# Two mixers of a two-layer trunk: subtracts moved from GpSimd to VectorE, queries rotated ahead of their norm, and output projections with two blocks to a bank

## The chip, the cores and the metric

The kernel runs on one core of a Trainium2 chip. A core has five engines, each with its own stream of instructions in a fixed order: TensorE (PE, with its weight load PEld), VectorE (DVE), ScalarE (ACT), GpSimd (POOL) and SyncE (SP, which here issues the DMAs). The metric is the device time of one execution in microseconds (us); lower is better.

## The reference, cut to what matters

A trunk of two layers over 256 tokens of width 1024, all in float32. Layer 0 mixes tokens by differential attention beside stick-breaking attention (one joint input projection, one joint output projection), layer 1 by multi-head latent attention (MLA). Each layer is a half feed-forward, the mixer, cross-attention to a memory of 256 tokens, and another half feed-forward.

```python
for layer in range(DEPTH):                                    # DEPTH = 2
    x = x + 0.5 * swiglu(rms_norm(x, ...), w_gate, w_up, w_down)   # width 2816
    h = rms_norm(x, mix_norm[layer])
    x = x + (diff_stickbreak_mixer(h, ...) if layer % 2 == 0 else mla_mixer(h, ...))
    x = x + memory_cross_attention(rms_norm(x, ...), rms_norm(mem, ...), ...)
    x = x + 0.5 * swiglu(rms_norm(x, ...), ...)
```

In both mixers, the mixed heads are multiplied by an output projection of 1024 x 1024. In MLA a query head is 96 wide; it is normed by its root mean square, and its last 32 values are rotated by their position. A rotation leaves the sum of squares as it is.

## The kernel before, in words

**Three passes.** A float32 product is made from high and low parts: a = hi + lo, and hi·hi + lo·hi + hi·lo is summed in PSUM by three matmuls (`mm3`, lines 285, 286 and 287 of the profile). A weight comes in through an SP DMA into `wr` (two buffers, `RAW`), ACT casts it to `wh` (line 250), and a subtract makes `wl` (line 252). The hi and lo tiles have three buffers (`HL`), so a weight's cast has to wait until PE has read the last of the weight three before it. In the mixers and the cross-attentions a weight of 128 x 2048 is cut into four pieces of 512 columns, p0 to p3, each with its own cast and subtract; DVE makes the subtract of the first three and POOL that of the last (`np_`, 512 columns). In the feed-forwards the pieces have 256 columns and all are DVE's.

**Order.** A planner (`run`) simulates tasks with priorities, tables of estimated durations (`EST_AB`, `EST_MLA`, `EST_X0`, `EST_X1`), times at which weights come and PSUM banks come free, and so fixes PE's order. The other engines' instructions are ordered by the scheduler of the framework; the update of the residual (`finish_dt`: x on DVE at line 511, xh on ACT at 482, xl on DVE at 483) has high priority there. Each engine then goes through its stream in order, and waits where an input or a buffer is not ready.

**Stages.** In us of the span: feed-forward up to 190, mixer of layer 0 ("AB") 190 to 329, its cross-attention to 368, two feed-forwards to 735, MLA 735 to 861, its cross-attention to 900, feed-forward to 1084.

**Output projection.** `out_g` makes eight blocks of 128 output columns out of four chunks of weights, chunk c holding blocks 2c and 2c+1. A block sums over eight rows of 128 (24 matmuls of 256 columns), in groups of two rows as the mixed heads become ready. A first window holds the first three blocks open in three PSUM banks and goes through them group by group, while the rest of the attention is made; then blocks 3 to 7 follow, one after the other. A block that is complete is added to x at once.

**MLA's queries.** `queries` takes each projected group of four heads for 128 tokens (n, t) from PSUM, squares it (ACT), sums the squares (DVE, 1350), adds the epsilon (1351), takes the reciprocal square root on POOL (468, four values a token), and rotates the last 32 values of a head: products with the tables on DVE (1358) and POOL (1360, two instructions), and their sum on DVE (1363). PE then transposes the queries (793), DVE copies them out of PSUM (1435), and the scores follow (1448).

Of the kernel before, what the change touches and what calls it, by code (L numbers as in the profile page):

```python
# [19 lines left out]
P = 128  # L20
S = 256
# [27 lines left out]
POOL_OF = {}  # L49
# [112 lines left out]
def trunk_kernel(ctx, tc, wflat, xT_d, xtok_d, memT_d, memtok_d, gains_d, rows_d, cst_d, out_d):  # L162
# [74 lines left out]
    def issue(i):  # L237
# [4 lines left out]
        np_ = 0 if name in ("gate", "up", "down") else POOL_OF.get(name, 512)  # L242
# [592 lines left out]
    def mem_k(l, c, events):  # L835
# [4 lines left out]
        def norm():  # L840
# [13 lines left out]
            yield dict(t=1, lat=7.0)  # L854
# [371 lines left out]
    def mixer_mla(gc):  # L1226
# [7 lines left out]
        rl, kk, kf, vt, kT, qf, rqs = {}, {}, {}, {}, {}, {}, {}  # L1234
# [103 lines left out]
        def queries(n, t, ps):  # L1338

            yield dict(after=[ev["rcq"]])  # L1340
            if t == 0:
                qf[n], rqs[n] = [], sl()
# [6 lines left out]
            v = sm()[:, 0:4]  # L1349
            V.tensor_reduce(out=v, in_=sq[:, 0:384].rearrange("p (a b) -> p a b", b=96), axis=AX.X, op=ALU.add)  # L1350
# [3 lines left out]
            tmp = al()  # L1354
            m1 = tmp[:, 0:128].rearrange("p (a b) -> p a b", b=32)
# [248 lines left out]
```

## Time and profile before

| | |
|---|---|
| time, median of 3 runs | 1088.73 us (1087.20 to 1089.23) |
| the profiled execution: time, span | 1086.18 us, 1084.5 us |
| busy over the span: PE, DVE, ACT, POOL | 1063.0, 769.4, 655.3, 192.4 us |

The span is what the trace covers; 1.7 us of the profiled execution's time lie around it. Busy time is the union of an engine's instructions, so a PE that is busy is not always at its full pace.

### The profile page before, as it was taken

The page shows a single profiled execution, that of the slowest core. Times are in us where ns is not written, and L with a number is a line of the kernel's source. Part 1 is how long each engine was busy: PE and PEld are TensorE (multiplying, and loading weights), DVE is VectorE, ACT ScalarE, POOL GpSimd, SP SyncE. Part 2 cuts the span into 40 slices and gives each one's busy share as a digit, 9 for nine tenths or more (in the row PEclk, how much of TensorE's full clock was granted, in tenths as well). Part 3 has the DMA queues.
Part 4 walks back from the last instruction along what each step waited for, and adds up shares of the span by engine and source line. Part 5 has one row for each costly group of instructions (what it writes and reads, how often), then busy time and mean ns, then how long its engine had stood idle before and what let it go on. Part 6 is the DMA issues. An engine that isn't in the chain of part 4 may idle for free.

```text
span 1084.5 us, 23380 instructions
## 1 busy us (share of the span) xinstructions
PE 1063.0 (98%) x9034; PEld 1044.5 (96%) x9034; DVE 769.4 (71%) x1866; ACT 655.3 (60%) x1775; POOL 192.4 (18%) x210
## 2 busy tenths in 40 slices
PE   8999999999899999999999999999989999999998
PEld 8999999998799999999999999999878999999998
DVE  5988765567867877776777777664688768777753
ACT  6766565567756665555666655565866567555542
POOL 0200001365434200000100000024861422000000
PEclk9999999999999999999999999999989999999999
DMA  8776556635345355555556565564341444555561
GB/s 285 247 250 218 197 191 206 195 89 184 99 136 195 119 193 196 193 185 199 200 189 220 200 208 184 182 197 158 97 147 49 155 150 164 195 195 195 185 225 58
DMA packets 51232, 193.36 MB, mean 178 GB/s; under 512 B 5808, under 2 KB 8368, under 8 KB 36016
## 3 DMA queue, kind: packets, MB, share of 16 engines
q1 hardware_dynamic: 50976, 191.81, 52.0%
q8 instruction: 71, 1.16, 0.4%
q14 instruction: 41, 0.34, 0.1%
q10 hardware_dynamic: 144, 0.05, 0.0%
HBM read 190.79 MB, written 1.05 MB: 177 GB/s over the span
## 4 chain that ended last, share of the span: by engine, by line
PE 90%; DVE 4%; ACT 2%; POOL 2%; issue 1%; DMA 1%; SPq 0%; DVEq 0%; ACTq 0%; POOLq 0%
PE mm L285 28%; PE mm L286 28%; PE mm L287 28%; DVE wl L252 1%; PE t L793 1%; ACT slotf L780 1%; POOL sm L468 1%; PE s L1448 1%; PE t L476 1%; DMA wr<-wflat 1%; PE s L918 0%; PE o L1481 0%; POOL sl L468 0%; PE s L285 0%; PE o L937 0%
## 5 line engine op out<-in xcount | busy, mean ns | idle before, releaser
L250 ACT CAST wh<-wr 128x256 fp32r<-128x256 f32 (+1 forms) x1216 | 441.0, 434 | 291.6 <-PE mm L286 234.2
L252 DVE TENSOR_TENSOR wl<-wr,wh 128x256 fp32r<-128x256 f32 (+1 forms) x1171 | 479.8, 466 | 125.6 <-ACT wh L250 120.2
L285 PE MATMUL mm<-xh,wh 128*128 128x256 f32 x1552 | 430.5, 277 | 1.9 <-ACT wh L271 1.9
L286 PE MATMUL mm<-xl,wh 128*128 128x256 f32 x1552 | 428.5, 276 | 0.0
L287 PE MATMUL mm<-xh,wl 128*128 128x256 f32 x1552 | 428.2, 276 | 0.0
L285 PEld LDWEIGHTS mm<-xh,wh 128*128 128x128 f32 x1552 | 292.3, 188 | 2.4 <-ACT wh L271 2.1
L286 PEld LDWEIGHTS mm<-xl,wh 128*128 128x128 f32 x1552 | 292.3, 188 | 0.6
L287 PEld LDWEIGHTS mm<-xh,wl 128*128 128x128 f32 x1552 | 292.1, 188 | 0.1
L285 PE MATMUL mm<-slotr,wh 128*128 128x256 f32 x896 | 247.6, 276 | 0.3 <-ACT slotr L482 0.3
L286 PE MATMUL mm<-slotr,wh 128*128 128x256 f32 x896 | 246.7, 275 | 0.4 <-DVE slotr L483 0.4
L287 PE MATMUL mm<-slotr,wl 128*128 128x256 f32 x896 | 246.6, 275 | 0.0
L285 PEld LDWEIGHTS mm<-slotr,wh 128*128 128x128 f32 x896 | 168.2, 188 | 1.0 <-ACT slotr L482 0.6
L286 PEld LDWEIGHTS mm<-slotr,wh 128*128 128x128 f32 x896 | 168.2, 188 | 0.7 <-DVE slotr L483 0.6
L287 PEld LDWEIGHTS mm<-slotr,wl 128*128 128x128 f32 x896 | 168.2, 188 | 0.0
L531 POOL TENSOR_TENSOR acc<-acc,sq 128x256 f32<-128x256 f32 x49 | 38.7, 789 | 452.5 <-ACT sq L523 450.4
L252 POOL TENSOR_TENSOR wl<-wr,wh 128x512 fp32r<-128x512 f32 x45 | 67.3, 1496 | 111.4 <-ACT wh L250 89.2
L739 DVE TENSOR_TENSOR slotf<-mm,rb 128x512 f32<-128x512 f32 x43 | 29.7, 690 | 53.7 <-PE mm L287 53.7
L482 ACT ACTIVATE xh<-x,gains 128x256 fp32r<-128x256 f32 x64 | 32.2, 507 | 27.8 <-DVE x L511 25.8
L780 ACT ACTIVATE slotf<-s,sm,sl 128x256 f32<-128x256 f32 (+1 forms) x64 | 32.7, 521 | 23.1 <-DVE sm L774 17.5
L729 DVE TENSOR_TENSOR slotf<-mm,rb 128x512 f32<-128x512 f32 x43 | 29.6, 689 | 21.0 <-PE mm L287 21.0
L511 DVE SCALAR_TENSOR_TENSOR x<-mm,x 128x256 f32<-128x256 f32 x64 | 26.8, 419 | 23.5 <-PE mm L287 23.5
L483 DVE SCALAR_TENSOR_TENSOR xl<-x,gains,xh 128x256 fp32r<-128x256 f32 x64 | 37.6, 592 | 5.7 <-ACT xh L482 5.5
(204 smaller groups left out, 1196.3 us busy)
## 6 DMA issues: line engine op xcount, KB each, us to landing
wr<-wflat SPq DMA_DIRECT2D x118, 1024.0 KB, 4.9
wr<-wflat SPq DMA_DIRECT2D x179, 256.0 KB, 3.9
wr<-wflat SPq DMA_DIRECT2D x16, 768.0 KB, 4.3
slotf<-memT SPq DMA_DIRECT2D x8, 256.0 KB, 3.4
wr<-wflat SPq DMA_DIRECT2D x2, 512.0 KB, 7.4
slotf<-xtok SPq DMA_DIRECT2D x4, 256.0 KB, 7.1
slotf<-memtok SPq DMA_DIRECT2D x4, 256.0 KB, 4.0
out<-x SPq DMA_DIRECT2D x8, 128.0 KB, 2.0
```

The costliest lines, as they stand in the source:

```text
L250: A.copy(hi[:, a:b], raw[:, a:b])
L252: e.tensor_tensor(out=lo[:, a:b], in0=raw[:, a:b], in1=hi[:, a:b].bitcast(F32), op=ALU.subtract)
L285: PE.matmul(out, a[0], b[0], start=first, stop=False, **kw)
L286: PE.matmul(out, a[0], b[1], start=False, stop=False, **kw)
L287: PE.matmul(out, a[1], b[0], start=False, stop=last, **kw)
L482: return (A.activation(hi, src, AF.Identity, scale=g), V.scalar_tensor_tensor(out=lo, in0=src, scalar=g, in1=hi.bitcast(F32), op0=ALU.mult ...
L483: V.scalar_tensor_tensor(out=lo, in0=src, scalar=g, in1=hi.bitcast(F32), op0=ALU.mult, op1=ALU.subtract))
L511: V.scalar_tensor_tensor(out=xd, in0=ps, scalar=factor, in1=xd, op0=ALU.mult, op1=ALU.add)
L531: G.tensor_tensor(out=st.acc, in0=st.acc, in1=sq, op=ALU.add)
L729: V.tensor_tensor(out=t.rearrange("p (a b) -> p a b", b=S), in0=pg.rearrange("p (a b) -> p a b", b=S), in1=rbb, op=ALU.mult)
L739: V.tensor_tensor(out=u.rearrange("p (a b) -> p a b", b=S), in0=pu.rearrange("p (a b) -> p a b", b=S), in1=rbb, op=ALU.mult)
L780: A.activation(p[:, i * w:(i + 1) * w], sps[:, i * w:(i + 1) * w], AF.Exp, bias=nb[:, i:i + 1], scale=r, accum_out=sums[:, i:i + 1])
```

## The change

Five edits. (1) All four pieces of a mixer's or cross-attention's weight are subtracted by DVE, none by POOL. (2) The first window of `out_g` holds six blocks, two to a bank in three banks; a pair is added to x when both its blocks are complete, and the last two blocks follow one by one (all four output projections of mixers and cross-attentions go through `out_g`). (3) In `queries` the rotation comes ahead of the sum of squares, its two intermediate products lie in unused columns of tiles that are there already, and one reciprocal square root of eight values replaces two of four. (4) Some of the planner's estimates are set anew. (5) In layer 0, the transposes of the memory's keys (`k0`, `k1`), which are made for the cross-attention during the mixer, are planned 9.0 after the projection rather than 7.0.

```diff
-POOL_OF = {}
-EST_X0 = {... 'o': 1.32, 'src': 8.83}
-EST_X1 = {... 'o': 1.18, 'src': 8.83}
-EST_AB = {... 'va': 1.47, ... 'sp': 3.0, ... 'srco': 1.25}
+EST_X0 = {... 'o': 1.6, 'src': 2.0}
+EST_X1 = {... 'o': 1.6, 'src': 2.0}
+EST_AB = {... 'va': 2.8, ... 'sp': 4.4, ... 'srco': 2.2}
...
-        np_ = 0 if name in ("gate", "up", "down") else POOL_OF.get(name, 512)
+        np_ = 0
...
+        nw = 2 * BANKS["mm"]
+        def bank(dt):
+            return dt // 2 * 2 if dt < nw else dt
...
+            b = bank(dt)
+            c0 = (dt - b) * S
             for i, k in enumerate(rows_):
-                mm3(pss[dt][:, 0:S], (w[0][:, k, j * P:(j + 1) * P], w[1][:, k, j * P:(j + 1) * P]),
-                    src[i], g == 0 and i == 0, g == len(groups) - 1 and i == len(rows_) - 1)
+                mm3(pss[b][:, c0:c0 + S], (w[0][:, k, j * P:(j + 1) * P], w[1][:, k, j * P:(j + 1) * P]),
+                    src[i], g == i == 0 and dt == b, g == len(groups) - 1 and i == len(rows_) - 1,
+                    skip_group_check=dt < nw)
...
-                ps = pss.pop(dt)
-                finish_dt(dt, gc, ps[:, 0:S])
-                drop(ps, 0.8)
-        nw = BANKS["mm"]
+                if dt >= nw or dt > b:
+                    for d in range(b, dt + 1):
+                        finish_dt(d, gc, pss[b][:, (d - b) * S:(d - b + 1) * S])
+                    drop(pss[b], 0.8)
...
-            yield dict(t=1, lat=7.0)
+            yield dict(t=1, lat=9.0 if l == 0 else 7.0)
...
-            v = sm()[:, 0:4]
-            V.tensor_reduce(out=v, in_=sq[...], axis=AX.X, op=ALU.add)
-            V.tensor_scalar(out=v, in0=v, scalar1=96 * EPS, scalar2=None, op0=ALU.add)
-            rsqrt(v, 4, rqs[n][:, t * 4:(t + 1) * 4])
...
             V.tensor_tensor(out=qr, in0=m1, in1=m2, op=ALU.add)
-            rel(sq, tmp)
+            V.tensor_reduce(out=qv[n][:, t * 4:(t + 1) * 4], in_=sq[...], axis=AX.X, op=ALU.add)
+            if t:
+                v = qv[n][:, 0:8]
+                V.tensor_scalar(out=v, in0=v, scalar1=96 * EPS, scalar2=None, op0=ALU.add)
+                rsqrt(v, 8, rqs[n])
+            rel(sq)
```

What the change does to the engines' streams shows at three places on DVE. In these rows a name's number is the tile, and the lines of the changed kernel lie 1 lower (up to 650) or 9 to 10 higher than those of the kernel before.

First, DVE in AB around the norm of the memory's first keys, `k0`. Before: lines 1197, 1198 and 1202 norm an attention output (o), 849, 850 and 853 norm `k0`, and POOL's reciprocal square roots stand between 1198 and 1202 and between 850 and 853.

```order
L1197 TENSOR_REDUCE sm_3861<-slotf_2674 128x4
L1164 SCALAR_TENSOR_TENSOR slotf_2658<-slotf_2664,sm_3845 128x256
L1198 TENSOR_SCALAR sm_3861<-sm_3861 128x4
L252 TENSOR_TENSOR wl_3890<-wr_3888,wh_3889 128x512
L1202 TENSOR_TENSOR slotf_2675<-o_3855,sm_3864 128x512
L849 TENSOR_REDUCE sm_3882<-slotf_2673 128x4
L252 TENSOR_TENSOR wl_3890<-wr_3888,wh_3889 128x512
L850 TENSOR_SCALAR sm_3882<-sm_3882 128x4
L252 TENSOR_TENSOR wl_3890<-wr_3888,wh_3889 128x512
L853 TENSOR_TENSOR slotf_2678<-slotf_2678,sm_3885 128x512
```

The changed kernel at the same norm (858, 859 and 862 are its three lines, 1206, 1207 and 1211 those of the attention output):

```order
L251 TENSOR_TENSOR wl_3848<-wr_3846,wh_3847 128x512
L858 TENSOR_REDUCE sm_3840<-slotf_2660 128x4
L251 TENSOR_TENSOR wl_3848<-wr_3846,wh_3847 128x512
L859 TENSOR_SCALAR sm_3840<-sm_3840 128x4
L251 TENSOR_TENSOR wl_3848<-wr_3846,wh_3847 128x512
L862 TENSOR_TENSOR slotf_2658<-slotf_2658,sm_3843 128x512
L251 TENSOR_TENSOR wl_3848<-wr_3846,wh_3847 128x512
L1206 TENSOR_REDUCE sm_3880<-slotf_2664 128x4
L1207 TENSOR_SCALAR sm_3880<-sm_3880 128x4
```

The norm of `k0` now stands ahead of that of the attention output, and four subtracts stand in the place of three.

Second, DVE in MLA from the second group of heads (n=1, both t) to the copies of the first transposed queries. Before:

```order
L1358 TENSOR_TENSOR slotf_9746<-slotf_9733,mqa 128x128
L1350 TENSOR_REDUCE sm_10369<-slotf_9745 128x4
L1363 TENSOR_TENSOR slotf_9733<-slotf_9746 128x4x32
L1351 TENSOR_SCALAR sm_10369<-sm_10369 128x4
L1358 TENSOR_TENSOR slotf_9734<-slotf_9737,mqa 128x128
L252 TENSOR_TENSOR wl_10426<-wr_10424,wh_10425 128x512
L1350 TENSOR_REDUCE sm_10404<-slotf_9742 128x4
L1363 TENSOR_TENSOR slotf_9737<-slotf_9734 128x4x32
L1351 TENSOR_SCALAR sm_10404<-sm_10404 128x4
L252 TENSOR_TENSOR wl_10426<-wr_10424,wh_10425 128x512
L1435 COPY slotf_9743<-t_10461 96x512
```

The changed kernel at the same place (1362, 1367, 1368, 1372 and 1445 are the lines of the product, the rotated sum, the sum of squares, the epsilon and the copy):

```order
L1362 TENSOR_TENSOR slotf_9734<-slotf_9734,mqa 128x128
L1367 TENSOR_TENSOR slotf_9734<-slotf_9734,slotf_9726 128x4x32
L1368 TENSOR_REDUCE sm_10357<-slotf_9726 128x4
L1362 TENSOR_TENSOR slotf_9740<-slotf_9740,mqa 128x128
L251 TENSOR_TENSOR wl_10414<-wr_10412,wh_10413 128x512
L1367 TENSOR_TENSOR slotf_9740<-slotf_9740,slotf_9744 128x4x32
L1368 TENSOR_REDUCE sm_10357<-slotf_9744 128x4
L1372 TENSOR_SCALAR sm_10357<-sm_10357 128x8
L251 TENSOR_TENSOR wl_10414<-wr_10412,wh_10413 128x512 x2
L1445 COPY slotf_9736<-t_10449 96x512
```

The rotation's sum moved ahead of the sum of squares, one epsilon stands for two, and a third subtract has come in ahead of the copy. On POOL, one reciprocal square root of eight values stands where two of four and a subtract stood.

Third, DVE in AB's output projection, from the split of the last mixed heads (483, `slotr`) on. Before, `wl_4098` is the weight of blocks 6 and 7, and `wl_4236` that of the cross-attention's queries:

```order
L483 SCALAR_TENSOR_TENSOR slotr_2682<-t_4143,small,slotr_2682 128x512
L511 SCALAR_TENSOR_TENSOR x<-mm_4082,x 128x256
L511 SCALAR_TENSOR_TENSOR x<-mm_4089,x 128x256
L483 SCALAR_TENSOR_TENSOR xl<-x,gains,xh 128x256
L511 SCALAR_TENSOR_TENSOR x<-mm_4111,x 128x256
L252 TENSOR_TENSOR wl_4098<-wr_4096,wh_4097 128x512
L483 SCALAR_TENSOR_TENSOR xl<-x,gains,xh 128x256 x2
L252 TENSOR_TENSOR wl_4098<-wr_4096,wh_4097 128x512 x2
L511 SCALAR_TENSOR_TENSOR x<-mm_4203,x 128x256
L252 TENSOR_TENSOR wl_4236<-wr_4234,wh_4235 128x512
```

The changed kernel, where `wl_4075` is the weight of blocks 6 and 7, and `mm_4060`, `mm_4088` and `mm_4138` are the banks of blocks 0 and 1, 2 and 3, 4 and 5:

```order
L482 SCALAR_TENSOR_TENSOR slotr_2682<-t_4194,small,slotr_2682 128x512
L510 SCALAR_TENSOR_TENSOR x<-mm_4060,x 128x256 x2
L251 TENSOR_TENSOR wl_4075<-wr_4073,wh_4074 128x512 x2
L510 SCALAR_TENSOR_TENSOR x<-mm_4088,x 128x256 x2
L482 SCALAR_TENSOR_TENSOR xl<-x,gains,xh 128x256
L510 SCALAR_TENSOR_TENSOR x<-mm_4138,x 128x256 x2
L482 SCALAR_TENSOR_TENSOR xl<-x,gains,xh 128x256 x5
L251 TENSOR_TENSOR wl_4075<-wr_4073,wh_4074 128x512 x2
L251 TENSOR_TENSOR wl_4125<-wr_4123,wh_4124 128x512 x4
```

The last two pieces of the last chunk now stand behind six updates of x and six subtracts of xl. In MLA the same stretch reads the same, row for row, with other tile numbers.

## Rows read from the trace of the kernel before

**Rows 1.** The page, parts 1 and 4: busy us (share) xinstructions, and the chain's shares.

```profile
PE 1063.0 (98%) x9034; PEld 1044.5 (96%) x9034; DVE 769.4 (71%) x1866; ACT 655.3 (60%) x1775; POOL 192.4 (18%) x210
...
PE 90%; DVE 4%; ACT 2%; POOL 2%; issue 1%; DMA 1%; SPq 0%; DVEq 0%; ACTq 0%; POOLq 0%
```

**Rows 2.** Windows: stretch, length, busy us (xinstructions) of each engine, PEclk, DMA.

```profile
190.00:320.00 130.00, 123.33 (x1051) 118.44 (x1051) 91.09 (x174) 84.33 (x192) 59.69 (x55) 1.00 0.43 139
...
380.00:735.00 355.00, 355.00 (x3132) 354.95 (x3131) 253.05 (x636) 207.21 (x596) 15.99 (x18) 1.00 0.57 196
735.00:850.00 115.00, 107.80 (x777) 98.24 (x778) 80.39 (x203) 75.91 (x180) 55.65 (x63) 0.97 0.34 111
```

**Rows 3.** Waits of PE, 190 to 320: us in total, times, longest.

```profile
PE t L793 <- DVE slotf L853: 2.3, 1, 2.3
PE s L323 <- ACT slotf L780: 1.9, 2, 1.0
PE o L1105 <- issue: 0.9, 1, 0.9
PE o L1105 <- ACT slotf L1017: 0.9, 1, 0.9
```

**Rows 4.** Waits of PE, whole span.

```profile
PE s L1448 <- DVE slotf L1435: 2.6, 1, 2.6
...
PE o L937 <- DVE slotf L801: 1.1, 2, 0.6
```

**Rows 5.** Timeline 290 to 298, DVE and PE: start, us, what, [idle before <- releaser].

```profile
292.17 0.69 DVE L1202 TENSOR_TENSOR slotf<-o,sm 128x512 f32<-128x512 f32 x1 [0.90 <-POOL sm L468]
292.78 0.68 DVE L849 TENSOR_REDUCE sm<-slotf 128x4 f32<-128x512 f32 x1
...
295.63 1.52 DVE L853 TENSOR_TENSOR slotf<-slotf,sm 128x512 f32<-128x512 f32 x1 [0.90 <-POOL sm L468]
...
297.29 0.63 PE L793 MATMUL t<-cst,slotf 128*128 128x128 f32 x4 [2.27 <-DVE slotf L853]
```

**Rows 6.** Timeline 783 to 792, DVE and PE, at MLA's first queries.

```profile
787.05 0.29 DVE L1363 TENSOR_TENSOR slotf<-slotf 128x128 f32<-128x128 f32 x1 [2.05 <-POOL slotf L1360]
...
789.68 0.29 DVE L1363 TENSOR_TENSOR slotf<-slotf 128x128 f32<-128x128 f32 x1 [1.00 <-POOL slotf L1360]
...
789.96 0.69 DVE L252 TENSOR_TENSOR wl<-wr,wh 128x512 fp32r<-128x512 f32 x1
790.56 1.28 DVE L1435 COPY slotf<-t 96x512 f32<-96x512 f32 x2
...
791.29 1.01 PE L1448 MATMUL s<-slotf,slotf 96*128 96x128 f32 x3 [2.64 <-DVE slotf L1435]
```

**Rows 7.** Windows of 5 us after that wait, columns as in rows 2.

```profile
790.00:795.00 5.00, 3.71 (x13) 3.30 (x14) 3.43 (x6) 2.01 (x4) 4.84 (x4) 0.59 0.39 120
795.00:800.00 5.00, 5.00 (x25) 4.84 (x24) 5.00 (x16) 3.39 (x13) 0.00 (x0) 0.73 0.47 170
```

**Rows 8.** Groups by shape, POOL, whole span: count, busy us, mean ns, idle before.

```profile
L252 POOL TENSOR_TENSOR wl<-wr,wh 128x512 fp32r<-128x512 f32 x45 | 67.3, 1496 | 111.4 <-ACT wh L250 89.2 <-PE mm L286 18.1 <-DMA wr<-wflat 4.1
```

**Rows 9.** Groups by shape, DVE: 190 to 320 (first), 735 to 850 (second).

```profile
L252 DVE TENSOR_TENSOR wl<-wr,wh 128x512 fp32r<-128x512 f32 x52 | 39.6, 793 | 8.3 <-ACT wh L250 8.2
...
L252 DVE TENSOR_TENSOR wl<-wr,wh 128x512 fp32r<-128x512 f32 x35 | 26.8, 784 | 11.9 <-ACT wh L250 11.9
```

**Rows 10.** Timeline 308 to 329, DVE and POOL, in AB's output projection.

```profile
313.46 0.42 DVE L511 SCALAR_TENSOR_TENSOR x<-mm,x 128x256 f32<-128x256 f32 x1 [2.34 <-PE mm L287]
...
315.21 0.68 DVE L252 TENSOR_TENSOR wl<-wr,wh 128x512 fp32r<-128x512 f32 x1
315.81 0.99 DVE L483 SCALAR_TENSOR_TENSOR xl<-x,gains,xh 128x256 fp32r<-128x256 f32 x2
...
321.31 2.98 DVE L252 TENSOR_TENSOR wl<-wr,wh 128x512 fp32r<-128x512 f32 x2 [0.71 <-ACT wh L250]
...
322.40 1.35 POOL L252 TENSOR_TENSOR wl<-wr,wh 128x512 fp32r<-128x512 f32 x1 [0.37 <-ACT wh L250]
```

More of the change, by code (lines that the diff above doesn't have):

```diff
@@ L58 @@
 PREADD = True
-EST_X0 = {'scale': 3.59, 'rq': 1.14, 'psd': 1.46, 'sp': 2.8, 'p1': 4.06, 'p2': 0, 'o': 1.32, 'src': 8.83}
-EST_X1 = {'scale': 2.31, 'rq': 1.14, 'psd': 1.46, 'sp': 2.8, 'p1': 3.39, 'p2': 0.0, 'o': 1.18, 'src': 8.83}
-EST_AB = {'b': 1.33, 'va': 1.47, 'rot': 14.92, 'st1': 6.44, 'st2': 0.14, 'z': 1.55, 'sto': 2.4, 'src': 0.79, 'T': 0.74, 'sp': 3.0, 'pc': 8.7, 'pcT': 1.4, 'po': 4.35, 'oa': 8.7, 'srco': 1.25}
+EST_X0 = {'scale': 3.59, 'rq': 1.14, 'psd': 1.46, 'sp': 2.8, 'p1': 4.06, 'p2': 0, 'o': 1.6, 'src': 2.0}
+EST_X1 = {'scale': 2.31, 'rq': 1.14, 'psd': 1.46, 'sp': 2.8, 'p1': 3.39, 'p2': 0.0, 'o': 1.6, 'src': 2.0}
+EST_AB = {'b': 1.33, 'va': 2.8, 'rot': 14.92, 'st1': 6.44, 'st2': 0.14, 'z': 1.55, 'sto': 2.4, 'src': 0.79, 'T': 0.74, 'sp': 4.4, 'pc': 8.7, 'pcT': 1.4, 'po': 4.35, 'oa': 8.7, 'srco': 2.2}
 PRIO_MLA = [1, 2, 4.2, 3.9, 4.4, 2.3]
@@ L678, in out_g @@
                 for dt in win:
-                    yield dict(after=[ev], w=keyf(dt // per), mm=int(g == 0))
+                    yield dict(after=[ev], w=keyf(dt // per), mm=int(g == 0 and dt == bank(dt)))
                     if dt // per not in ws:
                         ws[dt // per] = weight(keyf(dt // per), per * P)
-                    if g == 0:
+                    if g == 0 and dt == bank(dt):
                         pss[dt] = take("mm")
@@ L1233, in mixer_mla @@
         lat = {"ckv": ([], []), "cq": ([], [])}
-        rl, kk, kf, vt, kT, qf, rqs = {}, {}, {}, {}, {}, {}, {}
+        rl, kk, kf, vt, kT, qf, qv, rqs = {}, {}, {}, {}, {}, {}, {}, {}
         def latent(key, gc0, ps):
@@ L1341, in queries @@
             if t == 0:
-                qf[n], rqs[n] = [], sl()
+                qf[n], qv[n], rqs[n] = [], sm(), sl()
             z = al()
@@ L1348, in queries @@
             A.activation(sq[:, 0:384], z[:, 0:384], AF.Square)
-            v = sm()[:, 0:4]
-            V.tensor_reduce(out=v, in_=sq[:, 0:384].rearrange("p (a b) -> p a b", b=96), axis=AX.X, op=ALU.add)
-            V.tensor_scalar(out=v, in0=v, scalar1=96 * EPS, scalar2=None, op0=ALU.add)
-            rsqrt(v, 4, rqs[n][:, t * 4:(t + 1) * 4])
             qr = z[:, 0:384].rearrange("p (a b) -> p a b", b=96)[:, :, 64:96]
-            tmp = al()
-            m1 = tmp[:, 0:128].rearrange("p (a b) -> p a b", b=32)
-            m2 = tmp[:, 128:256].rearrange("p (a b) -> p a b", b=32)
+            m1 = z[:, 384:512].rearrange("p (a b) -> p a b", b=32)
+            m2 = sq[:, 384:512].rearrange("p (a b) -> p a b", b=32)
             ta, tb = tabs["mq"]
@@ L1363, in queries @@
             V.tensor_tensor(out=qr, in0=m1, in1=m2, op=ALU.add)
-            rel(sq, tmp)
+            V.tensor_reduce(out=qv[n][:, t * 4:(t + 1) * 4], in_=sq[:, 0:384].rearrange("p (a b) -> p a b", b=96),
+                            axis=AX.X, op=ALU.add)
+            if t:
[3 more added lines that the diff above has]
+            rel(sq)
             signal(ev["q", n, t], EST_MLA["q"])
```

## The prediction

> **What bounds the kernel now.** I read the page first. PE is busy for 98% of the span and makes 90% of the chain that ended last [rows 1], so only time in which PE waits, or runs slowly, can be won. The windows by stage say where that is. In the two feed-forwards from 380 to 735 PE never stops: 3132 matmuls in 355.00 us, 0.1133 us each [rows 2]. In AB it stands still for 130.00 - 123.33 = 6.67 us, in MLA for 115.00 - 107.80 = 7.20 us [rows 2]. The waits of PE name the causes. In AB they are 2.3 for the transposes of the memory's keys (L793 behind L853), 1.9 for scores that wait for a bank which a softmax still reads (L323), and 1.8 for L1105 [rows 3]. In MLA the longest is 2.6, L1448 behind L1435; the two cross-attentions have 1.1 together, L937 [rows 4]. PEclk is 1.00 in AB and in the feed-forwards, and 0.97 in MLA [rows 2]: behind the 2.64 us wait [rows 6], two stretches of 5 us have 0.59 and 0.73 [rows 7]. They mix full speed, 2.4 GHz, with 1.2 GHz, and lose 5 x 0.41 + 5 x 0.27 = 3.4 us. So at most about 14 + 3.4 us lie in what is touched.
>
> **Subtracts.** 45 of POOL's subtracts, 1496 ns each, go to DVE [rows 8]. Undisturbed, DVE takes 0.68 [rows 10]; 45 x 0.68 = 31 us more DVE work. Some comes back, since the DVE subtracts last 793 and 784 ns in the mean now [rows 9], and two beside a POOL subtract took 2.98 rather than 1.36, 1.6 more for a POOL instruction of 1.35 [rows 10]: 52 x 0.11 + 35 x 0.10 = 9 us. A third of the DVE rows is what moves: 17 pieces to AB (+11.6 - 5.7 = +6) and 12 to MLA (+8.2 - 3.5 = +5). DVE then is busy for 97 of 130 and 85 of 115 us, so it does not bound a stage by its sum; in MLA's softmaxes two more subtracts stand inside a chain that PE waits for. Bounds: 0 if they fall into gaps, 2 x 0.68 = 1.4 if both stand in the chain. I take **+0.7**. The Trainium skill, page "SBUF — State Buffer", section "Who interferes with whom", says that a VectorE instruction with two inputs in SBUF and a GpSimd instruction that reads SBUF exclude each other for a whole instruction. The 2.98 agrees; the means, 0.1 over the undisturbed value, say that it seldom happens. If every moved piece freed DVE for its whole 1.50, the +0.7 would become about 2 x (0.68 - 1.50) = -1.6, and the sum -5.8.
>
> **AB's waits.** Before, the norm of `k0` stood on DVE behind that of an attention output, whose last step waited 0.90 for POOL's reciprocal square root and held DVE from 292.17 to 292.78; only then came `k0`'s first step, its last ended at 297.15, and PE went on at 297.29 [rows 5]. In the changed order `k0`'s norm is ahead on DVE and on POOL: 0.90 + 0.61 are saved on DVE, and the POOL instruction, of about the 0.90 that is seen of it or more, no longer comes first. PE waited 2.27. The PE order puts 24 matmuls, 2.7 us, where 12 stood ahead of an L1105, and more matmuls between pairs of scores and their banks. All of 2.3 + 1.9 + 1.8 = 6.0 can go, at least 4 should, since the two largest have a definite replacement. I take **-5.5**.
>
> **MLA's queries.** Before, the rotated sums on DVE waited 2.05 and 1.00 for POOL, which had a reciprocal square root and a subtract in the queue ahead of the rotation; the copy L1435 stood behind them, and PE behind that [rows 6]. After the change the rotation waits for no reciprocal square root of its own group, and a third subtract comes ahead of the copy: -3.05 + 0.68 = -2.4, with 2.64 as its cap. I take **-2.3**; from below -1.0, if only the second wait goes. If PE then waits 0.3 rather than 2.64, what stood right ahead of the lower clock is gone, though PE pauses at other places of this stretch too (7.20 us in 115). Bounds 0 and -3.4; I take **-2.0**, nearer the second.
>
> **Output projections: a new wait.** The last chunk's hi and lo tiles are those of chunk 0, three weights back. Before, blocks 0 and 1 ended early, and PE had 78 matmuls of other blocks, 8.8 us, between the end of block 1 and its first use of the last chunk. Now chunk 0 is read until the last group of block 1. Call its end T. Only the last groups of blocks 2 to 5 are left then, 24 matmuls, 24 x 0.1133 = 2.7 us. DVE in order: x0 and x1, two subtracts of the last chunk (p0, p1), x2 and x3, one xl, x4 and x5, which exist at T + 2.7, then five xl, and only then p2 and p3. From T + 2.7: 0.1 to start, two x (0.7), five xl at 0.4 to 0.5 (2.2; two took 0.99 with their ends overlapping), p2 0.68 [rows 10]: T + 6.4. A piece holds two rows of the weight. In AB the groups go by rows 4 and 5 first, which are p2; PE would want it at T + 2.7 and waits **+3.7**. In MLA the groups go by rows 0 to 3 first, 12 matmuls, so PE wants p2 at T + 4.1 and waits **+2.3**. A wait of 0 is excluded as long as five xl stand ahead of p2. Bounds for each: 1.0 less, if x and xl follow one another closer than the rows show, and 0.7 more, if p3 is waited for as well. The pieces behind p3 are the next weight's, which PE wants 48 matmuls, 5.4 us, later, so the wait isn't passed on. The rest of the tail has no other gap to take it up.
>
> **Cross-attentions.** L937 waits 0.55 each time [rows 4]. In the first, eight casts and eight subtracts of the feed-forward's gate come ahead of the copy L801, so the wait stays and grows by some 0.2; in the second L801 stays first and the wait goes, behind 18 matmuls: **-0.4** together, from 0.5 to -1.1.
>
> The planner's estimates cost nothing themselves: they act through PE's order, counted above. SP issues the same DMAs in the same order; a raw buffer comes free when DVE's last piece ends rather than POOL's, which gains at a place without a DMA wait of PE's.
>
> **Sum.** +0.7 - 5.5 - 2.3 - 2.0 + 3.7 + 2.3 - 0.4 = -3.5 us. Against the profiled execution's own 1086.18 (1.7 of it around the span) that is 1082.7. This execution lies 2.55 below the median of the runs, 1088.73; the median to compare with is 1088.73 - 3.5 = **1085.2 us**.
>
> **Rivals.**
>
> *The tails cost nothing.* DVE reaches p2 in time, because PE's first two passes and a late turn of the last mixed heads leave more room than T + 2.7. Then 6.0 falls away: 1085.2 - 6.0 = 1079.2. Against it stands the written order of DVE's queue, which no duration in the rows shortens by 3 us. Chance 0.13.
>
> *The clock falls after the new waits; slower.* In MLA half speed came behind a wait of 2.64 and cost 3.4 [rows 6, 7]. The tail's waits are 3.7 and 2.3, each in a stretch where PE works on at once afterwards. If it falls behind the first alone, -3.5 + 3.4 = -0.1, 1088.6: no change. If it falls behind both, +3.3, 1092.0; it decides from there, and the point is the second wait, which is shorter than the one that was followed by half speed. For it: 3.7 is longer than any wait of PE's in the span [rows 4]. Against it: after AB's 2.27 [rows 5] the clock stayed at 1.00 [rows 2]. The Trainium skill, page "TensorE: Matmul & The Clock Gate", Part 1, says that the lower clock is the default and that activity lifts it, so that an idle stretch can bring it back; by that rule both tails are at risk, and a full PE before the wait protects it only in part. Chance 0.20 for the first alone, 0.08 for both.
>
> *AB's waits are moved, not closed.* The new order rests on estimates; DVE has 6 us more to do in AB, and a softmax or a norm that is late again holds PE elsewhere. With 1.5 won there rather than 5.5: +0.5, 1089.2, within the noise or a little slower. For it: three quarters of AB's waits are behind DVE or ACT chains that run through DVE. Chance 0.17.
>
> *The forecast*, 0.42, by itself 1082.5 to 1088.
>
> **How the numbers follow.** About 0.2%, 2.2 us, is what a measurement of this kernel can tell from no change. Faster by more: 0.34 of the forecast's 0.42 (the rest lies above 1086.5), the 0.13 without tails, and 0.05 of the others: 0.52. Slower: 0.08 with both clocks, 0.06 of the single fall with the tail waits at their upper bound, and 0.07 of the moved waits: 0.21. The rest, 0.27, is the same. The range goes from the hidden tails with MLA's clock held fully, 1078.5, to short of the case of both clocks, 1091.
>
> **What would show it.** Right: no POOL subtract is left and DVE's last 0.68 alone; no L793 wait behind the norm of the memory's keys; L1448 starts around 789 and PEclk is 1.00 from 790 to 800; a wait of PE for `wl` of 2 to 4 us in each mixer's output projection, at the matmul that uses p2 of the last chunk. Wrong: no such wait, or PEclk under 1.00 behind it; a PE wait behind a softmax in AB that isn't there now; DVE's busy time over 800 us.

## The result and the profile after

The changed kernel takes 1098.39 us (median of 4, 1097.3 to 1099.67) against 1088.36 us for the kernel before beside it: a ratio of 1.0093, with a 95% interval of 1.0076 to 1.0111. The prediction was 1085.2 us, in a range that ended at 1091. The change is slower by 10 us where a gain of 3.5 was forecast.

Part 1 of the page of the changed kernel, and two of its windows by stage, answer to [rows 1] and [rows 2]:

```profile
PE 1066.0 (97%) x9034; PEld 1047.6 (96%) x9034; DVE 781.4 (71%) x1908; ACT 656.5 (60%) x1775; POOL 126.3 (12%) x160
```

```profile
190.00:320.00 130.00, 126.81 (x1082) 121.87 (x1080) 91.32 (x190) 83.44 (x191) 32.70 (x37) 1.00 0.44 139
...
735.00:850.00 115.00, 106.75 (x787) 98.12 (x786) 85.00 (x209) 74.81 (x178) 39.85 (x48) 0.99 0.37 120
```

The loads moved the way that was worked out, DVE's by less: DVE went from 769.4 to 781.4 us, where 22 us more were worked out, and POOL from 192.4 to 126.3. The first window reads as a gain: PE is busy for 126.81 of 130 us rather than 123.33. So the loss is not there. The waits of PE over the span (us, times, longest) show where it is:

```profile
PE mm L286 <- DVE wl L251: 6.5, 3, 3.4
PE t L475 <- POOL acc L530: 3.9, 3, 1.8
...
PE t L802 <- DVE slotf L794: 2.3, 1, 2.3
PE t L802 <- DVE slotf L862: 1.8, 2, 1.5
PE t L802 <- POOL slotf L1325: 1.6, 1, 1.6
PE t L802 <- ACT slotf L1340: 1.6, 1, 1.6
PE t L475 <- ACT slotf L908: 1.5, 1, 1.5
...
PE s L1458 <- DVE slotf L1445: 1.0, 1, 1.0
```

Of the rows in [rows 3] and [rows 4], the waits for L1105, for the keys' norm in AB and for the scores' bank are gone, L1448's 2.64 and L937's two are gone, and two kinds have come that the kernel before did not have: for `wl`, and for `acc`, the sum of squares of the next norm (L475).

Since both kernels have the same 9034 matmuls and hold as many of them in each stage, the start of the n-th can be compared through the whole span. This table is made from the traces: the start in the kernel before, and how much later (+) or earlier (-) it is in each other kernel, all of them one profiled execution (e1 to e12 are the experiments below).

```
n     before    after      e1      e2      e3      e4      e5      e6      e7      e8      e9     e10     e11     e12
1900   224.90    0.49    0.54    0.08    0.00   -0.30   -0.01   -1.31   -0.14    0.96   -0.84   -1.28   -0.09    0.27
2620   316.21   -4.37    0.20    1.17   -2.32    1.20   -4.92   -6.13   -4.94   -3.85   -5.68   -2.49   -4.95   -4.60
2850   343.39    1.60    0.01    8.17   -2.51    1.23   -2.61   -2.49    3.34    2.12   -3.43    3.51    1.05   -2.61
3200   387.25    5.47    2.40   10.04   -2.76    1.19    4.57    0.96    3.53    4.51   -2.12    6.82    3.37   -0.69
6450   757.35    5.47    2.40   10.04   -2.76    1.19    4.57    0.96    3.53    4.51   -2.12    6.82    3.37   -0.69
7000   845.30    4.51    1.46    9.54   -3.33    0.55    2.52   -0.03    2.72    3.64   -4.17    6.04    2.80   -1.54
7700   929.64   11.69    2.54   20.22   -3.12    0.56   14.42   10.31    9.10   11.82   -1.03   17.01    9.88   -2.18
```

Between two rows lies a stretch: AB up to its output projection (1900 to 2620), the rest of that projection (to 2850), the first cross-attention's end (to 3200), two feed-forwards (to 6450), MLA up to its output projection (to 7000), and that projection with the second cross-attention (to 7700). For the changed kernel they give: AB -4.86, projection +5.97, cross-attention's end +3.87, feed-forwards 0.00, MLA -0.96, projection and cross-attention +7.18. What is before 1900 (+0.49) is the start of the program; it lies between -1.31 and +0.96 in the kernels of the table, with the same work there. The loss is 17 us at the two projections and the two cross-attentions, and the gain ahead of them 6.

**The first projection.** DVE and PE of the changed kernel (timeline), with T, the end of the last matmul that reads chunk 0, near 315.8:

```profile
315.90 0.76 DVE L510 SCALAR_TENSOR_TENSOR x<-mm,x 128x256 f32<-128x256 f32 x2 [5.07 <-PE mm L286]
316.57 1.28 DVE L251 TENSOR_TENSOR wl<-wr,wh 128x512 fp32r<-128x512 f32 x2
317.77 0.75 DVE L510 SCALAR_TENSOR_TENSOR x<-mm,x 128x256 f32<-128x256 f32 x2
318.44 0.48 DVE L482 SCALAR_TENSOR_TENSOR xl<-x,gains,xh 128x256 fp32r<-128x256 f32 x1
318.83 0.75 DVE L510 SCALAR_TENSOR_TENSOR x<-mm,x 128x256 f32<-128x256 f32 x2
319.49 2.06 DVE L482 SCALAR_TENSOR_TENSOR xl<-x,gains,xh 128x256 fp32r<-128x256 f32 x5
321.47 3.70 DVE L251 TENSOR_TENSOR wl<-wr,wh 128x512 fp32r<-128x512 f32 x6
```

```profile
322.21 0.39 PE L286 MATMUL mm<-slotr,wl 128*128 128x256 f32 x1 [3.37 <-DVE wl L251]
```

The queue stands as foreseen: p2 begins at 321.47 behind the five xl, and PE waits 3.37 for it. Behind that wait the clock fell from full speed (1.00) to half (0.50) for a time (windows of 2 us of the same kernel; the column after POOL's is PEclk):

```profile
322.00:324.00 2.00, 1.79 (x13) 1.79 (x14) 2.00 (x5) 1.42 (x4) 0.81 (x1) 0.87 0.05 15
324.00:326.00 2.00, 2.00 (x11) 2.00 (x11) 1.16 (x2) 0.21 (x1) 1.92 (x2) 0.50 0.88 206
326.00:328.00 2.00, 2.00 (x16) 2.00 (x15) 0.00 (x0) 1.21 (x4) 1.84 (x3) 0.78 0.90 303
```

It costs 2 x (0.13 + 0.50 + 0.22) = 1.7 us.

**The first cross-attention's end.** ACT, POOL and PE of the changed kernel, from the first block that is complete to the next norm:

```profile
365.94 0.40 ACT L522 ACTIVATE acc<-x 128x256 f32<-128x256 f32 x1
...
370.70 0.72 ACT L522 ACTIVATE sq<-x 128x256 f32<-128x256 f32 x2
...
372.90 0.42 ACT L522 ACTIVATE sq<-x 128x256 f32<-128x256 f32 x1 [0.47 <-POOL acc L530]
```

```profile
371.19 6.07 POOL L530 TENSOR_TENSOR acc<-acc,sq 128x256 f32<-128x256 f32 x7 [21.12 <-ACT sq L522]
```

```profile
377.31 0.61 PE L475 MATMUL t<-ones,acc 128*128 128x2 f32 x4 [1.80 <-POOL acc L530]
```

The first square is made at 365.94, the second only at 370.70, behind the xh of the other blocks and casts of the next weight; then POOL adds seven in a row, 0.87 each, and PE waits 1.80 for the last. There are two buffers for the squares, so that ACT makes each later one only when POOL has added an earlier one (the row at 372.90). The clock fell there too, to 0.52 and 0.63 in the next two windows of 2 us that PE fills: 1.7 us more. At the second cross-attention the same rows stand again (POOL from 911.21, 6.07 us), with a wait of 1.81, and there the clock held.

### The profile page after: what moved, and what is told of

Read it like the earlier page. It is cut to its first block, busy times and chain, and to the rows that moved or that the text cites. A ratio compares the mean times of both kernels' runs of the same rounds, so it can differ in the third digit from the quotient of the medians.

```text
span 1096.2 us, 23302 instructions
## 1 busy us (share of the span) xinstructions
PE 1066.0 (97%) x9034; PEld 1047.6 (96%) x9034; DVE 781.4 (71%) x1908; ACT 656.5 (60%) x1775; POOL 126.3 (12%) x160
## 4 chain that ended last, share of the span: by engine, by line
PE 60%; ACT 4%; DVE 3%; POOL 2%; issue 2%; DMA 1%; DVEq 0%; ACTq 0%
PE mm L284 19%; PE mm L286 19%; PE mm L285 19%; POOL acc L530 2%; ACT wh L249 2%; DVE wl L251 1%; PE t L802 1%; ACT slotf L789 1%; ACT xh L481 1%; DMA wr<-wflat 1%; POOL sm L467 1%; PE o L946 0%; PE s L1458 0%; PE s L927 0%; PE t L475 0%
## 5 line engine op out<-in xcount | busy, mean ns | idle before, releaser
L251 DVE TENSOR_TENSOR wl<-wr,wh 128x256 fp32r<-128x256 f32 (+1 forms) x1216 | 503.9, 473 | 130.8 <-ACT wh L249 126.8
L530 POOL TENSOR_TENSOR acc<-acc,sq 128x256 f32<-128x256 f32 x49 | 42.1, 858 | 534.5 <-ACT sq L522 532.9
L487 DVE TENSOR_TENSOR slotr<-slotf,slotr 128x512 fp32r<-128x512 f32 (+1 forms) x52 | 35.8, 689 | 3.4 <-ACT slotr L486 3.1
L284 PE MATMUL mm<-wh,mem 128*128 128x256 f32 x128 | 37.4, 292 | 0.0
```

The lines of the kernel that those rows point to most:

```text
L251: e.tensor_tensor(out=lo[:, a:b], in0=raw[:, a:b], in1=hi[:, a:b].bitcast(F32), op=ALU.subtract)
L284: PE.matmul(out, a[0], b[0], start=first, stop=False, **kw)
L487: V.tensor_tensor(out=lo, in0=src, in1=hi.bitcast(F32), op=ALU.subtract)
L530: G.tensor_tensor(out=st.acc, in0=st.acc, in1=sq, op=ALU.add)
```

## The experiments

Every kernel was timed in 3 rounds (e12 in 5), against the kernel before on the same chip.

**e1, the changed kernel with the old projection.** Edit: `out_g` of before in the changed kernel.

```diff
-        nw = 2 * BANKS["mm"]
+        nw = BANKS["mm"]
...
-                if dt >= nw or dt > b:
-                    for d in range(b, dt + 1):
-                        finish_dt(d, gc, pss[b][:, (d - b) * S:(d - b + 1) * S])
-                    drop(pss[b], 0.8)
+                ps = pss.pop(dt)
+                finish_dt(dt, gc, ps[:, 0:S])
+                drop(ps, 0.8)
```

> The changed kernel with the output projection of before (first window of three blocks, one to a bank, each added to x when complete). Theory A, the six-block window costs the time (by the curve of matmul times: 7.3 us in AB's tail, 3.4 at the end of the first cross-attention, 3.7 in MLA's tail, 3.4 at the second cross-attention, 18 in all, while the other edits win 7): about 1081 us, 1079 to 1084, no PE wait for POOL's acc over 0.5 us and no wl wait over 1 us in the tails. Theory B, the subtracts moved to DVE make DVE's queue late there: 1095 to 1099.

Measured: 1087.29 us, ratio 0.9998 (0.9988 to 1.0007). Theory B is out: without the window 10.5 us less stand against before. But the time is 6 us above theory A's. In the table AB's gain is gone (0.20 - 0.54 = -0.3 from 1900 to 2620): ahead of the last mixed heads PE now waits 2.0 us with a transpose for L1201 and 1.1 for L871, and in this execution the clock fell to half behind them, from 306.8 to 313.6 us, which is 3.4 us more. The first cross-attention's end costs +2.39. So the six-block window earns a part of AB's gain as well as costing what follows; the larger part of what e1 lost in AB is the clock's.

**e2, the kernel before with the new projection alone.** Edit on the kernel before, as in e1 with the signs turned:

```diff
-        nw = BANKS["mm"]
+        nw = 2 * BANKS["mm"]
...
+                if dt >= nw or dt > b:
+                    for d in range(b, dt + 1):
+                        finish_dt(d, gc, pss[b][:, (d - b) * S:(d - b + 1) * S])
```

> The kernel before with the new output projection alone (POOL still subtracts the last pieces). Theory A: 1088.4 + 14 to 20 = 1102 to 1108 us, with PE waits for wl in both tails and for POOL's acc at the end of both cross-attentions. Theory B: no more than 1091, since POOL still takes its subtracts.

Measured: 1104.05 us, ratio 1.0159 (1.0144 to 1.0174), as theory A has it, with POOL still making its subtracts. It waits 6.8 us for `wl` and 3.6 for `acc`. AB gains nothing (+1.1 from 1900 to 2620, with a fall of the clock of 1.7 at 297): without the new estimates the window brings only its cost.

**e3, all subtracts on DVE alone.** Edit on the kernel before:

```diff
-        np_ = 0 if name in ("gate", "up", "down") else POOL_OF.get(name, 512)
+        np_ = 0
```

> The kernel before with all subtracts on DVE alone. Theory A: 1086 to 1090 us; DVE busy about 780 us, POOL about 124. Theory B: 1096 or more, with PE waits for wl or for slots that DVE writes.

Measured: 1085.17 us, ratio 0.9981 (0.9971 to 0.9991): a gain of 2.6 us, so this edit isn't the loss. DVE is busy for 782.0 us and POOL for 124.2, as expected. In MLA the edit is worth 0.6 only. PE's waits there (735 to 850):

```profile
PE s L1448 <- DVE slotf L1435: 2.9, 2, 1.9
PE t L793 <- DVE slotf L853: 1.8, 2, 1.5
PE t L793 <- POOL slotf L1316: 1.6, 1, 1.6
PE t L793 <- DVE slotf L785: 1.2, 1, 1.2
```

No half clock is left in MLA (PEclk 1.00 from 735 to 850), which is worth the 3.4 us of before; most of it went into longer waits, since PE's idle time between its 6450th and its 7000th matmul is 9.67 us here and 7.20 before.

**e4, the rotation ahead of the norm alone.** Edit: `queries` of the change in the kernel before:

```diff
-            rsqrt(v, 4, rqs[n][:, t * 4:(t + 1) * 4])
...
             V.tensor_tensor(out=qr, in0=m1, in1=m2, op=ALU.add)
+            V.tensor_reduce(out=qv[n][:, t * 4:(t + 1) * 4], in_=sq[...], axis=AX.X, op=ALU.add)
+            if t:
...
+                rsqrt(v, 8, rqs[n])
```

> The kernel before with the queries rotated ahead of their norm alone. If the rotation works as the prediction had it: L1448's wait of 2.64 us falls under 1, PEclk is 1.00 from 785 to 800, and the time is 1083 to 1086 us. If the wait only moves to another instruction of MLA: 1087 to 1089, with the clock below 1.00 somewhere in MLA.

Measured: 1086.43 us, ratio 0.9984 (0.9975 to 0.9993): 1.4 us, between the two expectations. L1449, the L1448 of before, waits 0.8 rather than 2.6; but transposes wait 2.9 for L853 and 1.9 for L785, 0.5 each before, the clock falls at 803 us instead of 791 and costs 1.7 rather than 3.4; MLA's stretch gains 0.64 in the table.

**e5, the window's xl behind the last chunk's subtracts.** Edit on the changed kernel:

```diff
-        with tc.high_priority():
-            split(h, l, xd, gcol(gc + dt))
+        if late:                      # the blocks of the first window
+            split(h, l, xd, gcol(gc + dt))
+        else:
+            with tc.high_priority():
+                split(h, l, xd, gcol(gc + dt))
```

> The changed kernel, where the window's six xh and xl lose their high priority, so that on DVE the last chunk's four subtracts come ahead of them (the updates of x stay where they are). Theory C, the order of DVE's queue makes the tails' waits for wl: they fall from 3.4 and 2.2 us to under 0.5, the half clock behind the first one goes (1.7 us), and the time is 1098.4 - 3.5 - 1.7 - 2.2 = 1091 us, 1089 to 1094. Theory D, the buffers that come free late make them whatever the order: wl waits stay over 2 us, 1096 to 1099.

Measured: 1102.08 us, ratio 1.0133 (1.0108 to 1.0159), a time that neither theory had. Of what made the waits theory C is right: the 3.4 and 2.0 for p2 are gone, AB's projection (2620 to 2850) costs +2.31 rather than +5.97, and the clock stays up there. The edit doesn't let the buffers come free earlier, so D is out. But the scheduler now puts xl behind the next weight's pieces too, and the time is lost elsewhere, in waits for xl and in three falls of the clock, at 369, 867 and 912 us (3.4, 1.7 and 3.4 us):

```profile
PE mm L285 <- DVE xl L482: 9.1, 7, 2.7
...
PE mm L286 <- DVE wl L251: 1.8, 3, 1.1
```

**e6, the squares summed by DVE.** Edit on the changed kernel:

```diff
-            G.tensor_tensor(out=st.acc, in0=st.acc, in1=sq, op=ALU.add)
+            (V if ps is not None else G).tensor_tensor(out=st.acc, in0=st.acc, in1=sq, op=ALU.add)
```

> The changed kernel, where DVE rather than POOL adds up the squares of the output projections. Theory E, six blocks that end together give POOL seven adds of 0.87 us in a row, and L475 waits for the last: the waits of L475 for acc (3.9 us) go, with the half clock behind the one at 377 us (1.7): 1098.4 - 5.6 = 1092.8 us, 1091 to 1095. Theory F, the squares themselves are late on ACT: L475 still waits more than 2.5 us in all, 1096 to 1099.

Measured: 1099.79 us, ratio 1.0122 (1.0095 to 1.0149): a miss. PE waits longer for the sum, not shorter:

```profile
PE t L475 <- DVE acc L530: 7.9, 3, 3.0
```

The time is near the one that theory F gave, but the run doesn't settle between E and F. DVE makes the first add only at 369.67 us, where its square began at 366.66, and puts a subtract between each two adds, so that the sum is late in DVE's own queue. Moving the adds to DVE is no remedy; what POOL's pace and ACT's order each add to the wait stays open here.

**e7, the squares early.** Edit on the changed kernel:

```diff
-            A.activation(dst, xd, AF.Square)
+            with tc.high_priority():
+                A.activation(dst, xd, AF.Square)
...
-            sq = T("sq", [P, S], 2)
+            sq = T("sq", [P, S], 4)
```

> The changed kernel with the squares in high priority, so that ACT makes each right behind its xh, and four buffers for them rather than two; POOL still adds. By theory F L475's waits for acc fall under 1 us in all: 1093 us, 1091 to 1095. By theory E, POOL's 7 x 0.87 = 6.1 us from the first square on, they fall too, since the chain then starts some 5 us earlier (1092 to 1095); if neither, they stay and the time is 1096 or more. In AB a cast of the last chunk then stands behind five squares, which may lengthen the wait for wl by up to 1 us.

Measured: 1094.47 us, ratio 1.0061 (1.0043 to 1.0079), inside both ranges. The first cross-attention's end costs +0.19 rather than +3.87: POOL begins earlier and follows the squares,

```profile
368.47 0.75 POOL L531 TENSOR_TENSOR acc<-acc,sq 128x256 f32<-128x256 f32 x1 [16.71 <-ACT sq L523]
369.55 4.61 POOL L531 TENSOR_TENSOR acc<-acc,sq 128x256 f32<-128x256 f32 x5 [0.33 <-ACT sq L523]
```

and no wait for `acc` is among PE's. The order of the squares and the number of their buffers were changed together, and which of the two does it was not taken apart. In the mixers the same edit does harm, by more than the 1 us allowed for: the waits for `wl` are 10.0 us in all, with 4.8 and 4.1 for p2 in the two projections, and half clock behind each (3.4 us each time). It isn't the casts that stand behind squares: ACT casts p2 at 317.72, long before DVE subtracts it at 322.98. POOL's adds now run beside the five xl, and these take 3.94 us rather than 2.06:

```profile
317.72 0.60 ACT L249 CAST wh<-wr 128x512 fp32r<-128x512 f32 x1
...
319.11 3.94 DVE L482 SCALAR_TENSOR_TENSOR xl<-x,gains,xh 128x256 fp32r<-128x256 f32 x5
322.98 3.69 DVE L251 TENSOR_TENSOR wl<-wr,wh 128x512 fp32r<-128x512 f32 x6
...
319.19 3.58 POOL L531 TENSOR_TENSOR acc<-acc,sq 128x256 f32<-128x256 f32 x4 [0.95 <-ACT sq L523]
```

In MLA's projection the five xl and POOL's four adds read 3.94 and 3.58 again.

**e8, the old window in the cross-attentions.** Edit: `out_g` of before, under the name `out_1`, for the two cross-attentions only:

```diff
-            yield from out_g(lambda c: (f"xo{l}", c), 2,
+            yield from out_1(lambda c: (f"xo{l}", c), 2,
```

> The changed kernel with the window of three single blocks in the two cross-attentions' projections and that of six in the mixers'. If the two cross-attentions' ends cost what the curve says (3.4 and 3.4 us): 1098.4 - 6.8 = 1091.6 us, 1090 to 1094, no L475 wait at 377 and 917 us. If they cost little by themselves and the mixers' tails carry the loss: 1096 to 1099.

Measured: 1097.58 us, ratio 1.0085 (1.0065 to 1.0106): a miss. No wait for `acc` is left at 377 and 917, but PE now waits 2.2 us between 350 and 385 for the split of the last heads and for L842, 0.6 of which the changed kernel has too, so that its end costs +2.39 instead of +3.87, the difference being the clock, which didn't fall there. From 7000 to 7700 it loses more than the changed kernel, +8.18, with two falls of the clock, at 864 and 881 us, that cost 3.4 together and that the changed kernel's execution didn't have. So the old window takes the wait for `acc` away and wins nothing that the times can tell (1.0085 against 1.0093).

**e9, the orders put right.** Edit on the changed kernel: e5's in the mixers alone, e7's in the cross-attentions alone (the four buffers everywhere), and the weight after the last chunk is asked for one use later, so that its pieces stand behind the xl:

```diff
-        while issued[0] <= min(i + LOOK, len(plan) - 1):
+        while issued[0] <= min(i + (LOOK - 1 if key in (("ab_o", 2), ("mla_o", 2)) else LOOK), len(plan) - 1):
```

> The changed kernel with three changes of order and none of work: in the mixers' projections the last chunk's subtracts stand ahead of the window's xl, and these ahead of the next weight's subtracts; in the cross-attentions each square stands right behind its xh; and the squares have four buffers. If the orders of DVE's and ACT's queues are the whole loss at the ends of the projections (waits for wl 3.5 and 2.2, for acc 2.0, 2.0 and 1.7, two stretches of half clock of 1.7 each): 1098.4 - 13 = 1085 us, 1081 to 1088, with no PE wait over 1 us between 310 and 385 and between 840 and 925. If DVE simply has too much to do there, a wait for xl or for the next wl takes their place: 1092 or more.

Measured: 1085.77 us, ratio 0.9995 (0.9984 to 1.0005). The changed kernel was 10.0 us slower than the kernel before beside it; this one, with the same instructions in another order and two more buffers for the squares, is level with it: 1.1 below by the medians, with an interval of the ratio that includes 1. Its clock held from the start up to 1082 us. In the table the stretches that had lost 17.0 us lose 6.7 (2.25, 1.31 and 3.14), so about three fifths of the loss are gone. PE's waits of e9 from 310 to 385 (first), and from 840 to 925 (second):

```profile
PE mm L286 <- DVE wl L251: 1.3, 3, 0.7
PE t L809 <- DVE slotf L801: 0.7, 1, 0.7
PE mm L285 <- DVE slotr L487: 0.6, 1, 0.6
```

```profile
PE mm L286 <- DVE wl L251: 1.6, 1, 1.6
PE t L475 <- POOL acc L537: 0.8, 1, 0.8
```

The expectation that no wait over 1 us stays is missed by one, the 1.6 behind MLA's projection. The row that leads to it is DVE's, in MLA's tail:

```profile
853.38 2.72 DVE L482 SCALAR_TENSOR_TENSOR xl<-x,gains,xh 128x256 fp32r<-128x256 f32 x3
```

Three xl take 2.72 us beside POOL's adds, where five took 2.06 alone in the changed kernel at 319.49.

**e10, the old estimates.** Edit: the tables of before in the changed kernel:

```diff
-EST_AB = {... 'va': 2.8, ... 'sp': 4.4, ... 'srco': 2.2}
+EST_AB = {... 'va': 1.47, ... 'sp': 3.0, ... 'srco': 1.25}
...
-            yield dict(t=1, lat=9.0 if l == 0 else 7.0)
+            yield dict(t=1, lat=7.0)
```

> The changed kernel with the planner's estimates of before (and the memory's keys 7.0 after their projection). If the new estimates closed AB's waits: AB loses about 5 us again, 1103 us (1101 to 1105), with L1105's, L323's and the keys' waits back. If the six-block window did it, by giving PE work to put between: 1098 plus or minus 1.5.

Measured: 1102.66 us, ratio 1.0139 (1.0114 to 1.0165). From 1900 to 2620 it gains 1.2 rather than 4.9: 2.3 for the keys' norm, 0.8 for the scores' bank and 0.8 ahead of an L1114 (L1105 before) are back, and the clock fell behind the first of these (1.7). With e1: in AB, PE's idle time is 6.67 us before, 2.04 in the changed kernel, 4.37 with the old estimates and 3.77 with the old window. So the estimates and the window each carry a part of the gain, and the falls of the clock in e1 and e10 make what either loses look larger.

**e11, the old queries.** Edit: `queries` of before in the changed kernel, e4's with the signs turned:

```diff
-                rsqrt(v, 8, rqs[n])
...
+            rsqrt(v, 4, rqs[n][:, t * 4:(t + 1) * 4])
```

> The changed kernel with the queries normed ahead of their rotation, as before. If the rotation is what took the half clock out of MLA and shortened L1448's wait (2.64 to nothing, 1.7 us of clock): 1102 us, 1100 to 1104, PEclk under 0.9 near 790 to 800. If it only moved the wait: 1097 to 1100.

Measured: 1098.67 us, ratio 1.0111 (1.0083 to 1.0139), equal to the changed kernel. Within the whole change the rotation for the most part moves waits: without it L1457 (the L1448 of before) waits 1.2, and the transpose behind L794 1.1 less. PE's idle time in MLA (6450 to 7000) is 9.69 us here and 8.25 in the changed kernel, but here the clock held in all of MLA, near 790 too, and there it fell (1.7).

**e12, e9 with the old window in MLA.** Edit on e9, with `out_g` of before as `out_1` (the later request for a weight stays in AB alone):

```diff
-            yield from out_g(lambda c: ("mla_o", c), 4,
+            yield from out_1(lambda c: ("mla_o", c), 4,
```

> The kernel of e9 with the window of three single blocks in MLA's projection alone, so that the six-block window stays in AB and the cross-attentions. On the curve e9 loses 3.1 us between MLA's last matmuls and the second cross-attention (a wait for wl of 1.8, one for acc of 1.0). If the window is what makes these: 1085.8 - 3 = 1083 us, 1081.5 to 1085, 0.3 to 0.5% below before. If the old window of MLA leaves PE short of work ahead of the last mixed heads, as it did in AB with the new estimates (6 us): 1086 to 1090.

Measured, in 5 rounds: 1083.36 us, ratio 0.996 (0.9947 to 0.9974). This is faster than both kernels, by 4.1 us than the one before. In its profile the gain against e9 is where it was expected, -0.64 from 7000 to 7700 rather than +3.14.

## Why the prediction was wrong

It summed seven terms to -3.5; on the profiled spans the change is 1096.2 - 1084.5 = +11.7. The 15.2 between are worked out from the stretches of the table.

- **The new wait in the projections was right in place, cause and size, and its consequences were missed.** 3.7 and 2.3 were predicted, 3.4 and 2.0 are in the waits, for p2 as foreseen. e5 shows that the order of DVE's queue makes them. The step that failed here is "so the wait isn't passed on": a wait for xl of 0.6 came behind the same queue, and in AB the clock fell (1.7, the mechanism of the second rival at half its price): +5.97 for 3.7. PEclk under 1.00 behind this wait was one of the prediction's own signs of being wrong.
- **Not in the sum at all: the squares of the next norm.** Six blocks that end within a few microseconds hand six xh, six squares and seven adds to ACT and POOL at once. I followed DVE's queue and SP's, and neither ACT's squares nor POOL's adds. "-0.4 together" for the cross-attentions is the term that failed most. L937's waits went, both of them, but the first end costs +3.87 (wait 1.8 and its clock 1.7), and the second stretch +7.18 where 2.3 - 0.6 = 1.7 stood (`wl` 2.0, xl 0.7, `acc` 2.1 in two waits, and 1.5 for L908). L908 is on ACT behind a cast that waited 2.47 for a weight's DMA (row below), where the prediction had the DMAs touch no wait of PE's. e7 shows that squares which begin earlier, with two more buffers, take the wait for `acc` away at the cross-attentions, and e9 that the orders, with these buffers, carry 10.3 of the 17.0 us. Of the other 6.7, e12 wins 3.8 back with the old window in MLA; the rest was not taken apart. These two errors are 2.3 + 3.7 + 5.5 = 11.5 of the 15.2.

```profile
877.75 0.62 ACT L249 CAST wh<-wr 128x512 fp32r<-128x512 f32 x1 [2.47 <-DMA wr<-wflat]
```

- **MLA: -0.96 where 0.7 - 2.3 - 2.0 = -3.6 stood.** The rotation closed L1448's wait, and the clock at 790 held (it held there in e3 and e11 as well, behind 1.9 and 1.2). But the waits didn't go. By +0.7 and -2.3, PE's idle time in MLA (6450 to 7000) had to fall from 7.20 to 5.6 us; it is 8.25, and 8.17 with the rotation alone (e4), 9.67 with the subtracts alone (e3). A PE at half speed can cover waits that show at full speed (e9, whose clock held in MLA, has 8.45), so these sums give no price for each edit, and which of "+0.7", with 1.4 as its bound, and "-2.3" was mis-sized, and by how much, stays open. DVE just ahead of the wait of 2.3 in the changed kernel, and PE behind it:

```profile
808.48 0.68 DVE L251 TENSOR_TENSOR wl<-wr,wh 128x512 fp32r<-128x512 f32 x1
...
809.68 0.68 DVE L251 TENSOR_TENSOR wl<-wr,wh 128x512 fp32r<-128x512 f32 x1
...
810.41 0.69 DVE L251 TENSOR_TENSOR wl<-wr,wh 128x512 fp32r<-128x512 f32 x1
811.01 0.74 DVE L794 TENSOR_SCALAR slotf<-slotf,sm 128x256 f32<-128x256 f32 x2
```

```profile
811.48 0.86 PE L802 MATMUL t<-cst,slotf 128*128 128x128 f32 x3 [2.29 <-DVE slotf L794]
```

  Three subtracts, not two, stand between the steps of one chain, and PE waits for it; the clock falls here instead of at 790 and costs 2 x (0.11 + 0.50 + 0.25) = 1.7 between 810 and 816. The same transpose waits 0.5 before, 1.2 with the subtracts and without the rotation (e3, e11), and 1.9 with the rotation alone (e4), so both edits lengthen this wait. The clock's part came out at 3.4 - 1.7 = 1.7 for the 2.0 that stood, by luck: it held at one place and fell at another.
- **AB: -4.86 where -5.5 stood**; right, with its causes: PE's idle time there went from 6.67 to 2.04 us, 1.1 of which is a new wait for `wl` at 299. e1 and e10 add that the window and the estimates each carry a part of it.
- **Subtracts on DVE: no loss by themselves.** DVE's load grew by 12 us where 31 - 9 = 22 were worked out; e3 gives 2.6 us of gain for that edit alone. DVE's subtract fell from 793 and 784 ns in the mean [rows 9] to 710 and 714 in the changed kernel. That, the five xl of e7 that took 3.94 us beside POOL's adds and the three of e9 that took 2.72, agree with the exclusion that the Trainium skill, page "SBUF — State Buffer", section "Who interferes with whom", states.
- The rest is 0.5 at the program's start. A slip in the working: the lower end of the range, hidden tails with MLA's clock held fully, comes to 1085.2 - 6.0 - 1.4 = 1077.8 rather than 1078.5, which changes nothing here.

The rival of a wait that is merely moved got the wrong place (AB, 0.17): it was MLA. The case that came, new waits at the end of a stage behind work that is bunched, was in no rival.

## What to carry to other kernels

Keeping more blocks open to cover one wait makes them end together, and everything that follows a block (its update, its splits, its square, the sum, the release of its weight) then arrives as one burst on engines that go through their queues in order; so follow each of these queues to the next instruction that PE wants, before counting the gain. The same instructions in another order, with two more buffers, were worth 10 to 11 us here (from 10.0 above the kernel before to level with it, e9). Gains of a change in several parts don't add: the window was a loss of 16 us without the new estimates (e2), and the estimates and the other edits won nothing without the window (e1).

## What the runs showed of the hardware

Whether the clock falls behind a wait of PE does not follow from the wait's length. In one profiled execution of the changed kernel it fell behind waits of 3.37 (322), 1.80 (377) and 2.29 us (811), and held behind 2.05 (863) and behind 1.81 (917), the twin of the one at 377. The same wait goes either way from kernel to kernel: behind MLA's 2.29 us the clock fell in seven executions (the changed kernel, e1, e6, e7, e8, e10, e12) and held in two (e5, e9); behind p2's 3.36 in AB's projection it fell in e8 and e11 and held in e6; and behind the 2.2 to 2.3 of the keys' norm in AB, where the prediction took the held clock as an argument, it held before and in e3 and fell in e2, e4 and e10. The two windows of 2 us that PE fills first, at 378 and at 918:

```profile
378.00:380.00 2.00, 2.00 (x11) 2.00 (x11) 2.00 (x7) 0.00 (x0) 0.00 (x0) 0.52 0.71 180
```

```profile
918.00:920.00 2.00, 2.00 (x19) 2.00 (x19) 2.00 (x7) 0.00 (x0) 0.00 (x0) 1.00 0.56 147
```

11 matmuls against 19 after equal waits, behind the same instructions. What decides it is not shown. Each fall cost 1.7 us here and 3.4 in the kernel before [rows 7]; a sum for a single execution can be off by that for each such wait.

DVE's xl, an instruction with two tiles as inputs, ran at about half its pace beside adds on POOL: five xl took 2.06 us with POOL idle (the changed kernel at 319.49) and 3.94 beside four of POOL's adds (e7 at 319.11).
